# An encoder layer on one core: twelve of the last sixteen block moves issued from GpSimd's queue, and the planner may fill between the row halves of the embedding products

## The chip, the cores and the metric

The kernel runs on one core of a Trainium2 chip. The metric is the device time of one execution in microseconds. Three executions of the kernel before took 1150.88, 1150.77 and 1153.72 us; their median is 1150.88 us.

## The reference, cut to what matters

One layer with S = 256 rows and D = 2048 columns, in float32. Three sub-layers follow each other, each adding to the residual stream h: a mixing part (projections, attention, a recurrent scan, an output projection), a feed-forward part and an embedding part. Only the seam between the last two is touched:

```python
fn = rms_norm(h, g_ffn_pre)
ff = (silu(fn @ w_ffn_gate) * (fn @ w_ffn_up)) @ w_ffn_down
h = h + rms_norm(ff, g_ffn_post)
gate = sigmoid(rms_norm(h, g_ple_pre) @ w_ple_gate)   # 256x2048 times 2048x2048
ple = p @ w_ple_proj                                  # 256x256 times 256x2048
h = h + rms_norm(gate * ple, g_ple_post)
```

## The kernel before, in words

**Products.** Every float32 product is made of three products of split operands: a value is split in a high part (rounded) and a low part (the rest), and hi·hi, lo·hi and hi·lo are summed. A weight tile holds two blocks of 128 rows by 512 columns (512 KB). It is loaded from SyncE's queue into one of four buffers `wr`, ScalarE rounds it to `wh` (L637), VectorE subtracts to `wl` (L650), and TensorE runs 12 matmuls on it: 2 blocks × 2 halves of the rows × 3 products (L684 `wh` with the high part of the activations, L685 `wh` with the low part, L686 `wl` with the high part). A load into `wr` has to wait until the subtraction four tiles earlier has read that buffer; a rounding has to wait until TensorE has finished with the tile four earlier.

**The seam.** After the last feed-forward product come the embedding products for columns 1024 to 2047 (`embedding(2, "sm")` and `embedding(3)`: two tiles of `w_ple_proj`, left operand `pTh`/`pTl`), then the gate products with `w_ple_gate`. The gate's 32 weight tiles are called g0 to g31 in this text. g0 to g15 go in turns over two column chunks: g0 and g1 are the rows 0 to 255 of the weight for chunks 0 and 1, g2 and g3 the next 256 rows, and so on. So g12 to g15 use the last four of the sixteen blocks of the normed activations.

**The normed activations.** The gate's left operand is the transposed residual, times the gain, split in `hT_ffn_hi` (ScalarE, L316) and `hT_ffn_lo` (VectorE, L318), 16 blocks of 128 columns. `next_norm` computes h in pieces of 256 columns for each half of the rows (L1555, sixteen instructions). Blocks 0 to 11 are transposed on TensorE (`transposed`, L329, four matmuls for two blocks) into PSUM. Blocks 12 to 15 take another way (`turn_h`): VectorE transposes them in 32x32 squares into a tile `mid` (L1586), and 16 DMAs of 32 KB each (`moved`, L348) put the squares in their places in a tile `mT`; ScalarE and VectorE then split `mT`. The DMAs run over j (outer) and i (inner), four values each; `pool` lists the values of i whose DMAs GpSimd's queue issues, SyncE's queue issues the rest.

**What sets the order.** The program is written out by a planner. TensorE's main sequence calls `plan.main(cost)` to advance a modelled TensorE clock, and `plan.run()` to emit, in order of modelled start, all side work (roundings, splits, transposes, DMA issues) that would start before that clock. The order of the instructions on each engine is fixed when the program is built; at run time each engine goes through its own list in order and waits where an operand or a buffer is not ready. A queue is an engine's list too: a DMA that has to wait holds up all DMAs behind it on that queue.

Of the kernel before, what the change touches and what calls it, by code (L numbers as in the profile page):

```python
# [18 lines left out]
NT = S // P  # L19
# [61 lines left out]
class Event:  # L81


    t = None
# [141 lines left out]
def dve(n, take=None, give=None):  # L226
    return ("dve", COST["dve"] + 0.00104 * n, None, take, give)
# [11 lines left out]
def layer(ctx: ExitStack, tc: tile.TileContext, a: dict, out: bass.AP):  # L239
# [5 lines left out]
    plan = Plan(wr=R_BUFS, w=W_BUFS, sm=SM_BUFS, acc=4, ev=1, mid=2, bt=2, m2=1, mt=1, sq=1, T0=1, T1=1, T4=1, **{f"{s}{j}": n for s, m, n in (("p", 5, 1), ("t", 3, 0)) for j in range(m)}, wr0=1, w0=1)  # L245
# [52 lines left out]
    def col(name, i):  # L298
        c = VEC_COLS[name][0] + i
        return vec[:, c : c + 1]  # L300
# [13 lines left out]
    def gained_split(hi, lo, src, g, give=None):  # L314
        yield act(S)
        nc.scalar.activation(hi, src, AF.Copy, scale=g)  # L316
        yield dve(S, give=give)
        nc.vector.scalar_tensor_tensor(  # L318
            out=lo, in0=src, scalar=g, in1=f32(hi), op0=ALU.mult, op1=ALU.subtract
        )  # L320
# [11 lines left out]
    def moved(e, here, take, tile_of, turn=True, pool=()):  # L332


        if turn:
            flat = e.rearrange("p t n -> p (t n)")
            yield dve(2 * N)
            nc.vector.transpose(out=flat, in_=flat)
        src = e.rearrange("p t (k j b) -> p t k j b", j=4, b=32)
        mT = None  # L340
        for j in range(4):
            for i in range(4):
                first = None if mT else take
                yield ("pool" if i in pool else "dma", COST["move"], None, first, None)
                if mT is None:
                    mT = tile_of()
                dst = mT.rearrange("p t k (i b) -> p t k i b", b=32)
                (nc.gpsimd if i in pool else nc.sync).dma_start(  # L348
                    dst[32 * j : 32 * j + 32, :, :, i, :],
                    src[32 * i : 32 * i + 32, :, :, j, :],  # L350
                )
        done(here)
        return mT.rearrange("p t k q -> p k t q")
# [16 lines left out]
    def done(event):  # L370
        event.t = plan.now
# [148 lines left out]
    fours = {}  # L520

    raws, his, los = {}, {}, {}
    ev_raw, ev_hi, ev_lo = {}, {}, {}
# [138 lines left out]
    MM = 0.216  # L662
    MM4 = 0.86

    def products(i, kx, lhs, accs, ts, start, stop, *after, seeded=False):
        group = {"skip_group_check": seeded}
        for j in range(2):
            p = (i, j + 1) if (i, j + 1) in ev_lo else (i, 2)
            plan.reach(lhs.ev[kx + j])
            hi, lo = lhs.at[kx + j]  # L670
            st, sp = start and j == 0, stop and j == 1
            if i == 0:
                plan.main(4 * MM, ev_hi[p], lhs.ev[kx + j])
                for t in ts:
                    sl = slice(t * P, (t + 1) * P)
                    nc.tensor.matmul(accs[t], hi[:, sl], his[i][:, j, :], start=st, stop=False, **group)
                    nc.tensor.matmul(accs[t], lo[:, sl], his[i][:, j, :], start=False, stop=False, **group)
                plan.main(2 * MM, ev_lo[p])
            else:
                plan.main(6 * MM * len(ts) / NT, ev_lo[p], lhs.ev[kx + j], *after)  # L680
            for t in ts:
                sl = slice(t * P, (t + 1) * P)
                if i:
                    nc.tensor.matmul(accs[t], hi[:, sl], his[i][:, j, :], start=st, stop=False, **group)  # L684
                    nc.tensor.matmul(accs[t], lo[:, sl], his[i][:, j, :], start=False, stop=False, **group)  # L685
                nc.tensor.matmul(accs[t], hi[:, sl], los[i][:, j, :], start=False, stop=sp, **group)  # L686
            at_pe[0] = max(at_pe[0], i)
            if j:
                free_w(i)
            plan.run()  # L690
# [124 lines left out]
    def free_w(i):  # L815
        if i not in keep:
            plan.free[w_kind(i)].append(plan.clk["pe"])
        if i == max(more_w):
            plan.add(next_gain(("ffn", "g_ffn_post"), plan.clk["pe"]), plan.clk["pe"])

    keep = set()
    def run_seg(s):
        if callable(s[0]):
            s[0](*s[1:])
            return
        chunk, lhs, ks, first, last, after, i0 = s
        if after:
            after()
        if first:
            chunk.open()  # L830
        for n, (_, kx) in enumerate(ks):
            i = i0 + n
            before = [chunk.ready] if first and n == 0 else [chunk.made] if chunk.made else []
            products(i, kx, lhs, chunk.accs, range(NT), first and n == 0,
                     last and n == len(ks) - 1, *before, seeded=bool(chunk.made))
            his.pop(i), los.pop(i)
        if last:
            if chunk.before:
                chunk.before()
            plan.add(chunk.post(chunk), plan.clk["pe"] + plan.SEM, chunk.late)  # L840
            plan.run()
# [584 lines left out]
    pT = [Act(2)] * 2  # L1426
# [96 lines left out]
    def next_norm(sub, nxt, rstd, ev_rstd, g_next):  # L1523
# [24 lines left out]
        for c in range(4):  # L1548
            if c > 1:
                yield nxt.ev[4 * c - 8]  # L1550
            for b in range(2):
                sl = slice(c * N + b * S, c * N + (b + 1) * S)
                for t in range(NT):
                    yield dve(S)
                    nc.vector.scalar_tensor_tensor(  # L1555
                        out=h[:, t, sl], in0=mg[:, t, sl], scalar=ro[:, t : t + 1],
                        in1=h[:, t, sl], op0=ALU.mult, op1=ALU.add,
                    )
                if c < TURNED:
                    plan.add(transpose_h(4 * c + 2 * b, hi, lo, nxt, sub.gname), plan.now)  # L1560
            if c >= TURNED:
                plan.add(turn_h(c, hi, lo, nxt, sub.gname), plan.now, -SOON)
# [17 lines left out]
    def turn_h(c, hi, lo, nxt, gname):  # L1580

        for t in range(NT):
            yield dve(N, take=None if t else "mid")
            if not t:
                e = mid_tile()
            nc.vector.transpose(out=e[:, t, :], in_=t2["h"][:, t, c * N : (c + 1) * N])  # L1586
        there = Event()
        mT = yield from moved(e, there, "mt", mT_tile, turn=False)
        plan.free["mid"].append(plan.now)
        yield there  # L1590
        for b in range(4):
            kk = 4 * c + b
            yield from gained_split(
                *(x[:, kk, :].rearrange("p (t q) -> p t q", t=NT) for x in (hi, lo)), mT[:, b],
                col(gname, kk), give="mt" if b == 3 else None,
            )
            done(nxt.ev[kk])
# [106 lines left out]
    hP = Act()  # L1704
# [16 lines left out]
    def mid_tile():  # L1721
        return t2["pool"].tile([P, NT, N], F32, tag="mid", name="mid", bufs=2)
# [138 lines left out]
    for part, (f0, f1) in enumerate(PARTS):  # L1861
# [11 lines left out]
        for c in range(0, 4, 2):  # L1873
# [11 lines left out]
                after=load_sqrt if end else None,  # L1885
# [172 lines left out]
    n = 0  # L2058
# [47 lines left out]
    with tc.manual_schedule():  # L2106
# [3 lines left out]
        for n, s in enumerate(segs[:-1]):  # L2110
# [3 lines left out]
            if n == n_ffn:  # L2114
                MM = 0.2265
# [7 lines left out]
        chunk, lhs, ks, _, _, _, i0 = segs[-1]  # L2123
        chunk.open()
        for n, (_, kx) in enumerate(ks):
            products(i0 + n, kx, lhs, chunk.accs, [0], n == 0, n == 7, chunk.ready)
# [73 lines left out]
```

## Time and profile before

| what | value |
|---|---|
| three executions, median | 1150.88 us (1150.77 to 1153.72) |
| the profiled execution: time, span of its instructions | 1153.04 us, 1151.0 us |
| TensorE busy, of the span | 1140.0 us, 99% |
| VectorE, ScalarE, GpSimd busy | 79%, 62%, 12% |
| granted TensorE clock, mean | 0.999 |
| bytes moved by DMA | 266.92 MB, mean 232 GB/s |

Times in the views count from the start of the span. Between the profiled execution's own time and its span lie 2.04 us. In the timeline a row is one instruction, or several alike with their count; a bracket at its end gives the idle time of the engine before it and what ended it. Matmuls overlap, so their pace is read from the starts of successive rows and not from their durations. "SPq" and "POOL" rows with DMA_DIRECT2D are issues; the time from an issue to the arrival of its data is given as "DMA to landing".

### The profile page before, as it was taken

The page shows a single profiled execution, that of the slowest core. Times are in us where ns is not written, and L with a number is a line of the kernel's source. Part 1 is how long each engine was busy: PE and PEld are TensorE (multiplying, and loading weights), DVE is VectorE, ACT ScalarE, POOL GpSimd, SP SyncE. Part 2 cuts the span into 40 slices and gives each one's busy share as a digit, 9 for nine tenths or more (in the row PEclk, how much of TensorE's full clock was granted, in tenths as well). Part 3 has the DMA queues.
Part 4 walks back from the last instruction along what each step waited for, and adds up shares of the span by engine and source line. Part 5 has one row for each costly group of instructions (what it writes and reads, how often), then busy time and mean ns, then how long its engine had stood idle before and what let it go on. Part 6 is the DMA issues. An engine that isn't in the chain of part 4 may idle for free.

```text
span 1151.0 us, 15131 instructions
## 1 busy us (share of the span) xinstructions
PE 1140.0 (99%) x5211; PEld 947.9 (82%) x5211; DVE 909.9 (79%) x1143; ACT 714.4 (62%) x948; POOL 135.3 (12%) x216
## 2 busy tenths in 40 slices
PE   9999999999999999999999999999999999999997
PEld 7888888888888888888888888888888888887786
DVE  6578787888458779988787898988888888759574
ACT  6777877875457645656656556565555565556564
POOL 0000000000000033131100123311111303100000
PEclk9999999999999999999999999999999999999999
DMA  9867666546686996876976786887887687965671
GB/s 325 283 191 219 185 185 206 174 148 206 226 285 178 313 296 212 259 199 213 279 253 221 249 237 211 264 254 207 290 291 256 196 264 249 284 237 203 207 246 75
DMA packets 112573, 266.92 MB, mean 232 GB/s; under 512 B 39280, under 2 KB 46192, under 8 KB 111088
## 3 DMA queue, kind: packets, MB, share of 16 engines
q1 hardware_dynamic: 99568, 243.57, 62.8%
q0 software_dynamic: 12496, 22.03, 9.7%
q8 instruction: 41, 0.67, 0.2%
q10 hardware_dynamic: 432, 0.35, 0.1%
q14 instruction: 36, 0.29, 0.1%
HBM read 248.07 MB, written 9.44 MB: 224 GB/s over the span
## 4 chain that ended last, share of the span: by engine, by line
PE 93%; DMA 2%; DVE 2%; ACT 2%; issue 1%; SPq 0%; ACTq 0%; DVEq 0%
PE acc L685 24%; PE acc L686 24%; PE acc L684 24%; PE acc L696 6%; PE acc L695 6%; PE acc L697 6%; PE tr L329 1%; DVE wl L650 1%; ACT wh L637 1%; DMA sq<-ev 0%; DMA mT<-mid 0%; DMA wr<-in_w_ple_gate 0%; PE pg L360 0%; PE pg L361 0%; DMA av<-in_w_rg_i 0%
## 5 line engine op out<-in xcount | busy, mean ns | idle before, releaser
L650 DVE TENSOR_TENSOR wl<-wr,wh 128x1024 fp32r<-128x1024 f32 (+1 forms) x308 | 368.2, 1210 | 106.9 <-ACT wh L637 104.9
L637 ACT CAST wh<-wr 128x1024 fp32r<-128x1024 f32 (+1 forms) x308 | 318.9, 1043 | 198.9 <-PE acc L685 139.2
L685 PE MATMUL acc<-wh,hT_mix_lo 128*128 128x512 f32 x440 | 171.4, 390 | 0.3 <-DVE hT_mix_lo L318 0.3
L684 PE MATMUL acc<-wh,hT_mix_hi 128*128 128x512 f32 x440 | 171.5, 390 | 0.0
L686 PE MATMUL acc<-wl,hT_mix_hi 128*128 128x512 f32 x440 | 171.2, 389 | 0.0
L348 POOL DMA_DIRECT2D mT<-mid x152 | 89.5, 602 | 559.8 <-DMA ple<-in_w_ffn_up 401.2
L686 PE MATMUL acc<-wl,hT_hi 128*128 128x512 f32 x320 | 124.5, 390 | 0.0
L684 PE MATMUL acc<-wh,hT_hi 128*128 128x512 f32 x316 | 124.4, 394 | 0.0
L685 PE MATMUL acc<-wh,hT_lo 128*128 128x512 f32 x316 | 123.1, 390 | 0.0
L637 ACT CAST wh<-ple 128x1024 fp32r<-128x1024 f32 (+1 forms) x61 | 59.8, 982 | 64.5 <-PE acc L685 30.8
L685 PEld LDWEIGHTS acc<-wh,hT_mix_lo 128*128 128x128 f32 x440 | 82.6, 188 | 18.0 <-DVE hT_mix_lo L318 1.0
L686 PEld LDWEIGHTS acc<-wl,hT_mix_hi 128*128 128x128 f32 x440 | 82.6, 188 | 17.1
L684 PEld LDWEIGHTS acc<-wh,hT_mix_hi 128*128 128x128 f32 x440 | 82.6, 188 | 17.0
L650 DVE TENSOR_TENSOR wl<-ple,wh 128x1024 fp32r<-128x1024 f32 (+1 forms) x61 | 69.1, 1133 | 9.3 <-ACT wh L637 8.7
L686 PEld LDWEIGHTS acc<-wl,hT_hi 128*128 128x128 f32 x320 | 60.1, 188 | 12.9
L685 PEld LDWEIGHTS acc<-wh,hT_lo 128*128 128x128 f32 x316 | 59.4, 188 | 11.7
L684 PEld LDWEIGHTS acc<-wh,hT_hi 128*128 128x128 f32 x316 | 59.4, 188 | 11.3
L637 ACT CAST wh<-third 128x1024 fp32r<-128x1024 f32 x32 | 33.6, 1051 | 21.0 <-PE acc L685 18.8
L650 DVE TENSOR_TENSOR wl<-third,wh 128x1024 fp32r<-128x1024 f32 x32 | 39.1, 1221 | 6.8 <-ACT wh L637 6.6
L606 POOL DMA_DIRECT2D ple<-in_w_ffn_up x27 | 24.0, 891 | 163.5 <-DVE wl L650 97.6
L684 PE MATMUL acc<-wh,hT_ffn_hi 128*128 128x512 f32 x104 | 40.9, 393 | 1.5 <-ACT hT_ffn_hi L316 1.5
L685 PE MATMUL acc<-wh,hT_ffn_lo 128*128 128x512 f32 x104 | 40.8, 393 | 0.5 <-DVE hT_ffn_lo L318 0.5
(439 smaller groups left out, 2386.9 us busy)
## 6 DMA issues: line engine op xcount, KB each, us to landing
wr<-in_w_in SPq DMA_DIRECT2D x77, 512.0 KB, 4.5
wr<-in_w_ffn_gate SPq DMA_DIRECT2D x74, 512.0 KB, 5.4
wr<-in_w_ffn_down SPq DMA_DIRECT2D x63, 512.0 KB, 5.2
wr<-in_w_ffn_up SPq DMA_DIRECT2D x49, 512.0 KB, 5.2
wr<-in_w_out SPq DMA_DIRECT2D x32, 512.0 KB, 4.4
wr<-in_w_ple_gate SPq DMA_DIRECT2D x32, 512.0 KB, 4.6
lower<-in_w_ffn_up SPq DMA_DIRECT2D x21, 512.0 KB, 6.1
third<-in_w_ffn_gate SPq DMA_DIRECT2D x14, 512.0 KB, 6.4
```

The lines of the kernel that those rows point to most:

```text
L329: nc.tensor.transpose(tr[:, b, t * P : (t + 1) * P], e[:, t, sl], ident)
L348: (nc.gpsimd if i in pool else nc.sync).dma_start(dst[32 * j : 32 * j + 32, :, :, i, :], src[32 * i : 32 * i + 32, :, :, j, :],)
L606: nc.gpsimd.dma_start(dst, src, accum_op=ALU.add)
L637: nc.scalar.copy(his[i][:, 0 : src.shape[1], :] if n == 2 else his[i][:, j, :], src)
L650: nc.vector.tensor_tensor(out=los[i][:, m, :], in0=src, in1=f32(his[i][:, m, :]), op=ALU.subtract)
L684: nc.tensor.matmul(accs[t], hi[:, sl], his[i][:, j, :], start=st, stop=False, **group)
L685: nc.tensor.matmul(accs[t], lo[:, sl], his[i][:, j, :], start=False, stop=False, **group)
L686: nc.tensor.matmul(accs[t], hi[:, sl], los[i][:, j, :], start=False, stop=sp, **group)
L695: nc.tensor.matmul(dst, x[0], wh, start=start, stop=False, skip_group_check=seeded)
L696: nc.tensor.matmul(dst, x[1], wh, start=False, stop=False, skip_group_check=seeded)
L697: nc.tensor.matmul(dst, x[0], wl, start=False, stop=stop, skip_group_check=seeded)
```

## The change

Two edits. In `turn_h`, where the norm feeds the gate (`nxt is hP`), the 12 DMAs with i = 0, 1, 2 are issued from GpSimd's queue, and only the four with i = 3 stay on SyncE's. The same step of the first norm (`hF`) stays as it was. In `products`, the modelled cost of a block is booked in two halves, one for each half of the rows, and for the embedding products behind the last feed-forward product (`lhs in pT and i > max(fours)`) `plan.run()` is called between the halves, so that side work can be emitted there.

```diff
             else:
-                plan.main(6 * MM * len(ts) / NT, ev_lo[p], lhs.ev[kx + j], *after)
-            for t in ts:
+                plan.main(6 * MM / NT, ev_lo[p], lhs.ev[kx + j], *after)
+            for n, t in enumerate(ts):
+                if i and n:
+                    if lhs in pT and i > max(fours):
+                        plan.run()
+                    plan.main(6 * MM / NT)
                 sl = slice(t * P, (t + 1) * P)
...
         there = Event()
-        mT = yield from moved(e, there, "mt", mT_tile, turn=False)
+        mT = yield from moved(e, there, "mt", mT_tile, turn=False, pool=(0, 1, 2) if nxt is hP else ())
```

The two programs are alike up to the seam. In the changed one, line numbers behind `products` are 4 higher, and what was L1555 is L1559; no computing instruction is added or removed, only the order and the issuing queue change.

SyncE's queue, from the load of the gate gain to the end of the gate's weight loads, before:

```order
L562 DMA wr<-in_w_ple_gate 128x1024 x2
L348 DMA mT<-mid 32x8x32 x3
L562 DMA wr<-in_w_ple_gate 128x1024 x2
L348 DMA mT<-mid 32x8x32
L562 DMA wr<-in_w_ple_gate 128x1024 x3
L348 DMA mT<-mid 32x8x32 x8
L562 DMA wr<-in_w_ple_gate 128x1024 x4
L348 DMA mT<-mid 32x8x32 x3
L562 DMA wr<-in_w_ple_gate 128x1024
L348 DMA mT<-mid 32x8x32
L562 DMA wr<-in_w_ple_gate 128x1024 x15
```

And the same stretch of the changed program:

```order
L562 DMA wr<-in_w_ple_gate 128x1024 x3
L348 DMA mT<-mid 32x8x32
L562 DMA wr<-in_w_ple_gate 128x1024
L348 DMA mT<-mid 32x8x32
L562 DMA wr<-in_w_ple_gate 128x1024 x3
L348 DMA mT<-mid 32x8x32 x2
L562 DMA wr<-in_w_ple_gate 128x1024 x20
```

The first row of each is g5 onwards. The last of the 16 moves stood behind the load of g16 and stands now behind that of g11; between the loads of g11 and g12 stand two moves where there were eight, and none between those of g15 and g17 where there were four. GpSimd's queue ends with 20 moves in a row instead of 8.

VectorE, from the first piece of h in the seam to the first low part of a turned block; before there were six pieces of h ahead of the first `wl` (that of g1), in the changed program three:

```order
L1559 SCALAR_TENSOR_TENSOR h_8470<-mg_8281,ro_ffn,h_8470 128x256
L1559 SCALAR_TENSOR_TENSOR h_8560<-mg_8359,ro_ffn,h_8560 128x256
L1559 SCALAR_TENSOR_TENSOR h_8470<-mg_8281,ro_ffn,h_8470 128x256
L650 TENSOR_TENSOR wl<-wr,wh 128x1024
L1559 SCALAR_TENSOR_TENSOR h_8560<-mg_8359,ro_ffn,h_8560 128x256
L1559 SCALAR_TENSOR_TENSOR h_8470<-mg_8281,ro_ffn,h_8470 128x256
L1559 SCALAR_TENSOR_TENSOR h_8560<-mg_8359,ro_ffn,h_8560 128x256
L318 SCALAR_TENSOR_TENSOR hT_ffn_lo<-tr,vec,hT_ffn_hi 128x256
```

Further on, between the first piece of h and the two 32x32 transposes of `turn_h`, VectorE has now three `wl` and ten low parts where it had two and eight. Behind the transposes the changed program has this (the first four `wl` are those of g4 to g7, the next two those of g8 and g9):

```order
L650 TENSOR_TENSOR wl<-wr,wh 128x1024
L318 SCALAR_TENSOR_TENSOR hT_ffn_lo<-tr,vec,hT_ffn_hi 128x256 x2
L650 TENSOR_TENSOR wl<-wr,wh 128x1024 x3
L1576 TENSOR_REDUCE toth_ffn<-ssh_ffn 128x2
L368 RECIPROCAL rstd_p<-rth_ffn 128x2
L650 TENSOR_TENSOR wl<-wr,wh 128x1024
L318 SCALAR_TENSOR_TENSOR hT_ffn_lo<-mT,vec,hT_ffn_hi 128x256 x3
L650 TENSOR_TENSOR wl<-wr,wh 128x1024
L318 SCALAR_TENSOR_TENSOR hT_ffn_lo<-mT,vec,hT_ffn_hi 128x256
```

Before, the four low parts of `mT` stood behind the `wl` of g13; now three of them stand ahead of the `wl` of g9. On ScalarE, likewise, the first `hT_ffn_hi` from `mT` stood behind the rounding of g13 and stands now ahead of that of g10. On TensorE, the 12 transposes ahead of the first gate matmul are now 8, and the rest stand in groups of 8, 4 and 4 where they stood in groups of 4 and 8; between the embedding products themselves no transpose stands in either program.

## The prediction

> **What bounds the kernel now.** First the page, its busy times and the chain that ended last:
>
> ```profile
> PE 1140.0 (99%) x5211; PEld 947.9 (82%) x5211; DVE 909.9 (79%) x1143; ACT 714.4 (62%) x948; POOL 135.3 (12%) x216
> PE 93%; DMA 2%; DVE 2%; ACT 2%; issue 1%; SPq 0%; ACTq 0%; DVEq 0%
> ```
>
> TensorE is the bound nearly throughout. The change neither adds nor removes a matmul, so all it can save is time in which TensorE waits. The view of waits, for TensorE over the whole span (us in total, times, longest):
>
> ```profile
> PE final L2042 <- ACT diag L2040: 2.0, 1, 2.0
> PE acc L684 <- ACT hT_ffn_hi L316: 1.5, 1, 1.5
> ...
> PE acc L685 <- DVE hT_ffn_lo L318: 0.5, 1, 0.5
> ...
> ```
>
> Two of them lie in the seam: 1.5 us for `hT_ffn_hi` and 0.5 us for `hT_ffn_lo`. The first is the one that the moved DMAs concern. TensorE's timeline at g2 and g12:
>
> ```profile
> 1057.72 0.39 PE L684 MATMUL acc<-wh,hT_ffn_hi 128*128 128x512 f32 x1
> ...
> 1084.73 0.39 PE L686 MATMUL acc<-wl,hT_ffn_hi 128*128 128x512 f32 x1
> 1086.60 0.50 PE L684 MATMUL acc<-wh,hT_ffn_hi 128*128 128x512 f32 x1 [1.48 <-ACT hT_ffn_hi L316]
> 1087.12 0.50 PE L685 MATMUL acc<-wh,hT_ffn_lo 128*128 128x512 f32 x1
> 1087.45 0.39 PE L686 MATMUL acc<-wl,hT_ffn_hi 128*128 128x512 f32 x1
> ```
>
> From 1057.72 to 1084.73 lie 119 matmul steps (g2 to g11 are ten tiles of 12), so a step is 0.227 us and a tile 2.72 us. At that pace the third matmul of g12 would start at 1084.73 + 3 × 0.227 = 1085.41; it starts at 1087.45. The wait thus costs **2.04 us**, the restart of the pipeline included.
>
> Who makes it late? SyncE's queue and ScalarE in the timeline:
>
> ```profile
> 1059.67 1.91 SPq L348 DMA_DIRECT2D mT<-mid  x3
> 1061.69 1.00 SPq L562 DMA_DIRECT2D wr<-in_w_ple_gate  x2
> 1062.74 1.20 SPq L348 DMA_DIRECT2D mT<-mid  x1
> 1064.25 4.28 SPq L562 DMA_DIRECT2D wr<-in_w_ple_gate  x3
> 1068.58 5.94 SPq L348 DMA_DIRECT2D mT<-mid  x8
> 1074.62 2.10 SPq L562 DMA_DIRECT2D wr<-in_w_ple_gate  x4
> 1076.77 1.94 SPq L348 DMA_DIRECT2D mT<-mid  x3
> 1081.07 0.33 SPq L562 DMA_DIRECT2D wr<-in_w_ple_gate  x1
> 1081.45 0.58 SPq L348 DMA_DIRECT2D mT<-mid  x1
> 1086.03 0.91 ACT L316 ACTIVATE hT_ffn_hi<-mT,vec 128x256 fp32r<-128x256 f32 x2 [4.99 <-DMA mT<-mid]
> ```
>
> The 16 moves are issued over 21.8 us, because each weight load between them waits for its buffer. The last leaves at 1081.45, and ScalarE can read `mT` at 1086.03, about 4.5 us later.
>
> **Part 1: the moved DMAs.** The 12 issues on GpSimd's queue depend on no weight load. When are all 16 there? Three terms.
>
> *Start.* The moves wait for VectorE's two 32x32 transposes. Rows of VectorE:
>
> ```profile
> 1046.16 2.46 DVE L1555 SCALAR_TENSOR_TENSOR h<-mg,ro_ffn,h 128x256 f32<-128x256 f32 x6
> 1048.55 1.22 DVE L650 TENSOR_TENSOR wl<-wr,wh 128x1024 fp32r<-128x1024 f32 x1
> 1049.68 0.48 DVE L1555 SCALAR_TENSOR_TENSOR h<-mg,ro_ffn,h 128x256 f32<-128x256 f32 x1
> 1050.08 0.48 DVE L318 SCALAR_TENSOR_TENSOR hT_ffn_lo<-tr,vec,hT_ffn_hi 128x256 fp32r<-128x256 f32 x1
> 1058.33 1.30 DVE L1586 STREAM_TRANSPOSE mid<-h 128x512 f32<-128x512 f32 x2
> ```
>
> From start to start a `wl` takes 1.13 us (1048.55 to 1049.68), a piece of h or a low part 0.40. The changed order puts one more `wl` and two more low parts ahead of the transposes: 1.13 + 2 × 0.40 = 1.93 us. The first move, at 1059.67 before, comes at about 1061.6.
>
> *Issue.* Bursts of moves on GpSimd's queue exist elsewhere in the trace; two of them, each with the time from issue to landing of its moves, and then the DMA share of the windows:
>
> ```profile
> 954.73 2.97 POOL L348 DMA_DIRECT2D mT<-mid  x5 [19.74 <-DVE sums L312]
> 957.90 5.17 POOL L348 DMA_DIRECT2D mT<-mid  x9 [0.20 <-issue]
> ```
>
> ```profile
> DMA to landing us min/median/max: 1.9/4.1/8.3
> ```
>
> ```profile
> 402.93 5.35 POOL L348 DMA_DIRECT2D mT<-mid  x9 [401.17 <-DMA ple<-in_w_ffn_up]
> ...
> 412.32 0.58 POOL L348 DMA_DIRECT2D mT<-mid  x1 [0.78 <-DMA mT<-mid]
> ```
>
> ```profile
> DMA to landing us min/median/max: 4.5/6.9/8.7
> ```
>
> ```profile
> 400.00:420.00 20.00, 20.00 (x90) 16.58 (x89) 15.51 (x18) 9.38 (x10) 10.40 (x17) 1.00 1.01 293
> 953.00:968.00 15.00, 15.00 (x68) 12.43 (x67) 14.12 (x14) 7.76 (x9) 10.33 (x17) 1.00 0.75 221
> 1059.00:1074.00 15.00, 15.00 (x68) 12.32 (x67) 10.78 (x16) 10.89 (x24) 0.00 (x0) 1.00 0.76 224
> ```
>
> The last figure but one is the DMA share: 0.75 in the first burst, 1.01 in the second, and 0.76 before in the window that now takes the moves. In the first burst 14 issues go in 8.3 us, 0.59 each, with no wait to speak of; the 12th leaves 11 × 0.59 = 6.5 us after the first, at 1068.1. In the second, issues wait for the landing of earlier moves, and the 12th leaves 9.4 us after the first (412.32). I take the first, since its DMA share is the same as here.
>
> *Landing.* 4.1 us is the median of the first burst, 6.9 that of the second. I take 5.0, nearer the first, because the weight loads of g9 to g11 fall on the end of the burst. So `mT` is complete at 1068.1 + 5.0 = **1073.1**. The four moves left on SyncE's queue end earlier: the last stands behind the load of g11, issued at the latest in the x3 row of 1064.25, so before 1068.6, plus two issues and 4.5 us, about 1073 too.
>
> g12 needs its first block at 1085, 12 us later. The wait there is gone: **−2.04 us**.
>
> *What is late next.* The planner has put the splits of `mT` early in two lists. On ScalarE the first `hT_ffn_hi` from `mT` stands ahead of the rounding of g10; on VectorE three low parts stand ahead of the `wl` of g9. Both engines stand still until `mT` is complete, and g8 is the last tile that doesn't need them. The cost of each step, from ScalarE's rows (starts: split to rounding 0.41, rounding to split 0.94):
>
> ```profile
> 1087.79 0.50 ACT L316 ACTIVATE hT_ffn_hi<-mT,vec 128x256 fp32r<-128x256 f32 x1
> 1088.20 1.04 ACT L637 CAST wh<-wr 128x1024 fp32r<-128x1024 f32 x1
> 1089.14 0.50 ACT L316 ACTIVATE hT_ffn_hi<-mT,vec 128x256 fp32r<-128x256 f32 x1
> ```
>
> From complete `mT`: split 0.41, rounding of g10 0.94, two splits 0.82, the third low part 0.48, `wl` of g9 1.13, and about 0.3 for the hand-overs between engines: 4.1 us. So `wl` of g9 is there at 1073.1 + 4.1 = 1077.2. g9 starts at 1057.72 + 7 × 2.72 = 1076.8, and its third matmul, the first with `wl`, at 1077.2. It is a dead heat: every microsecond that `mT` is later than 1073.1 becomes a wait of TensorE. I book 0.3 us of wait and 0.3 for the restart (the restart at g12 cost 2.04 − 1.48 = 0.56): **+0.6 us**. Ends: 0 (landing 4.1), and with the second burst's figures 1061.6 + 9.4 + 6.9 + 4.1 = 1082.0, a wait of 4.8 + 0.56 = +5.4 us.
>
> A row against a rule: the issue on SyncE's queue took 21.8 us for 16 moves, more than four times the landing of one. The Trainium skill (DMA: Bandwidth & Descriptors, Issuing engines are not separate DMA queues) says that transfers started by different engines run on the same 16 DMA engines, and that issuing from several saves only issue time, usually small beside the transfer. By that rule nothing would be gained; the rows above disagree on "small", since here the queue holds issues behind waiting loads.
>
> **Part 2: the finer steps of the planner.** No transpose comes to stand between the embedding products, but the orders differ after them. The `wl` of g1 stands 3 × 0.41 = 1.2 us earlier on VectorE, three pieces of h 1.13 us later. TensorE's side:
>
> ```profile
> 1048.40 1.47 PE L329 MATMUL tr<-ident,h 128*128 128x128 f32 x12
> ...
> 1050.61 0.50 PE L685 MATMUL acc<-wh,hT_ffn_lo 128*128 128x512 f32 x1 [0.50 <-DVE hT_ffn_lo L318]
> ```
>
> The first low part now stands behind six pieces of h and one `wl`, 1046.16 + 2.46 + 1.13 = 1049.75, and behind its high part, which ScalarE gives only after the rounding of g3; that rounding waits for the end of the embedding products at 1048.40, so the high part is there at 1048.40 + 0.94 + 0.41 = 1049.75 too. The low part ends near 1050.3 where it ended at 1050.08 + 0.48 = 1050.56, and L685 starts about 0.1 earlier: −0.1. But 16 transposes are then left where 12 were: 4 × 1.47 / 12 = +0.5. From 1050.61 to 1057.72 TensorE has 23 matmuls (5.2 us) and 12 transposes (1.5) in 7.1 us, so 0.4 of gaps; I let half of them close, since the low parts of later blocks now have more transposes ahead of them: −0.2. Net **+0.2 us**, between −0.3 (all gaps close and half of the transposes cost nothing extra) and +0.7 (one more wait of 0.5, like the one now). The rest of what moves is VectorE and ScalarE work that this case gives slack of over a microsecond: the `wl` of g2, behind the low part of block 6, comes near 1056.3 and is read at 1058.2.
>
> **Sum.** −2.04 + 0.6 + 0.2 = −1.2 us. After g12 the program is as before and TensorE is without a wait until `diag`, so the end moves by the same. Profiled: 1153.04 − 1.2 = 1151.8 us. The profiled execution lies 2.16 us above the median of the three runs; against that median the forecast is 1150.88 − 1.2 = **1149.7 us**. 0.3% of it is 3.45 us, about what a measurement of this kernel can tell from no change.
>
> **The rivals.**
>
> *A. The DMA engines hold the moves (0.20).* If the moves share busy engines, issuing earlier brings them no sooner than about 1074.5 to 1075; g9 then waits 1.4 to 1.9 us plus 0.5. For it: the share of 0.98 in the middle of the window,
>
> ```profile
> 1064.00:1069.00 5.00, 5.00 (x24) 4.14 (x23) 2.94 (x4) 3.93 (x12) 0.00 (x0) 1.00 0.98 346
> ```
>
> against it, the median of 4.1 us at a share of 0.75. It gives −2.04 + 2.2 + 0.2 = +0.4: 1151.3 us. This is also what is left of the rule above.
>
> *B. Slower: a new wait at g9 (0.15).* The mechanism is the split of `mT` standing ahead of g9's `wl`. It decides from `mT` complete at 1075.0 on. With the second burst's waits between issues and its landing, 1077.9, the sum is +5.4 − 2.04 + 0.2 = +3.6: 1154.5 us. Two thirds of this case lie above 0.3%.
>
> *C. The runs without a profile don't have the wait at g12 (0.14).* Their median is 2.16 us under the profiled execution, as much as the wait costs; with moves landing 2 us sooner it would be gone already. Then nothing is gained and the seam costs 0 to +0.8: about 1151.2 us. Against it: one of the three runs, 1153.72, is as slow as the profiled one, so the difference can have any origin.
>
> *D. More is gained than the waits show (0.03).* All waits of the seam with restarts and gaps are about 3.4 us; that would reach 1147.5 us.
>
> The forecast (−2.4 to −0.5) has 0.48. Range: from 1148.3 (no new wait, and the seam 0.5 better) to 1153.6, which takes in A, C and the lower part of B and leaves out about 0.12 above and 0.05 below. Faster by over 0.3%: 0.03 (D); slower: 0.10 (two thirds of B); within: 0.87.
>
> **What would show it.** Right: no wait of TensorE for `hT_ffn_hi` at g12, the first L348 of the seam on GpSimd near 1061.6, the last near 1068, the first split of `mT` near 1073, g9 with a wait under 1 us. Wrong: a wait of L686 for `wl` of over 2 us at g9 or g10, issues on GpSimd with idle times for earlier moves, or a span that is unchanged though TensorE waits less.

## The result, and the profile after

Over nine executions each, the kernel before has a median of 1151.96 us (1150.56 to 1153.72) and the changed kernel 1154.91 us (1152.92 to 1156.78). The ratio is 1.0023, 95% interval 1.0014 to 1.0032: the change makes the kernel slower, by 3 us. The prediction, 1149.7 us, a little faster, was wrong, and the result lies outside its range.

The profiled execution of the changed kernel is the fastest of the nine: 1152.92 us, span 1151.1 us. It reached the seam 0.62 us sooner than the profiled one of before (the first transposes behind the embedding products start at 1047.78 and 1048.40 us), so differences are taken from that point on.

The page's busy times of the changed kernel; the computing engines do what they did, GpSimd has the twelve issues more:

```profile
PE 1140.0 (99%) x5211; PEld 948.6 (82%) x5211; DVE 909.0 (79%) x1143; ACT 715.0 (62%) x948; POOL 142.2 (12%) x228
```

The waits of TensorE over the whole span, changed kernel (lines of `products` are 4 higher, so L688 to L690 were L684 to L686):

```profile
PE acc L690 <- DVE wl L650: 2.4, 1, 2.4
PE final L2046 <- ACT diag L2044: 2.0, 1, 2.0
...
```

The wait of 1.5 us for `hT_ffn_hi` at g12 is gone. A wait of 2.4 us for `wl` has come. TensorE's timeline shows its place:

```profile
1047.78 1.17 PE L329 MATMUL tr<-ident,h 128*128 128x128 f32 x8
1049.22 0.50 PE L688 MATMUL acc<-wh,hT_ffn_hi 128*128 128x512 f32 x1 [0.27 <-ACT hT_ffn_hi L316]
...
1056.93 0.40 PE L688 MATMUL acc<-wh,hT_ffn_hi 128*128 128x512 f32 x1
...
1076.21 0.39 PE L689 MATMUL acc<-wh,hT_ffn_lo 128*128 128x512 f32 x1
1078.99 0.50 PE L690 MATMUL acc<-wl,hT_ffn_hi 128*128 128x512 f32 x1 [2.39 <-DVE wl L650]
...
1141.87 1.02 PE L2141 MATMUL final<-h,ident 128*128 128x512 f32 x2
```

The row of 1056.93 is the first matmul of g2. Seven tiles of 2.72 us later is 1075.97, where g9 starts, so 1078.99 is the third matmul of g9, the first with g9's `wl`. It should have followed 0.23 us after 1076.21; the delay is 2.55 us. Now the issues of the changed kernel, SyncE's queue:

```profile
1060.68 0.60 SPq L348 DMA_DIRECT2D mT<-mid  x1
...
1063.70 2.61 SPq L562 DMA_DIRECT2D wr<-in_w_ple_gate  x3
1066.36 1.26 SPq L348 DMA_DIRECT2D mT<-mid  x2
1070.52 27.11 SPq L562 DMA_DIRECT2D wr<-in_w_ple_gate  x11
```

and GpSimd's:

```profile
1061.22 0.59 POOL L348 DMA_DIRECT2D mT<-mid  x1 [69.81 <-ACT wh L637]
1061.99 4.59 POOL L348 DMA_DIRECT2D mT<-mid  x8 [0.18 <-issue]
1067.17 1.73 POOL L348 DMA_DIRECT2D mT<-mid  x3 [0.59 <-DMA mT<-mid]
```

The sixteen moves leave between 1060.7 and 1068.3, where the last left at 1081.45 before. Three answers on the tile `mT` give their landing: the first is over all sixteen, the second over the last two of SyncE's queue (issued at 1066.4 and 1067.0), the third over the last three of GpSimd's (1067.2 to 1068.3):

```profile
DMA to landing us min/median/max: 2.7/5.9/8.2
```

```profile
DMA to landing us min/median/max: 7.8/8.0/8.2
```

```profile
DMA to landing us min/median/max: 6.1/6.5/6.9
```

Both queues end together: 1067.0 + 7.8 = 1074.8 and 1068.3 + 6.1 to 6.9 = 1074.4 to 1075.2 (the split below starts at 1075.03). The windows around it, in the columns used in the prediction:

```profile
1060.00:1065.00 5.00, 5.00 (x24) 4.14 (x23) 5.00 (x8) 3.94 (x9) 3.60 (x7) 1.00 0.82 215
1065.00:1070.00 5.00, 5.00 (x24) 4.14 (x23) 2.01 (x4) 4.77 (x13) 3.31 (x6) 1.00 1.05 287
1070.00:1075.00 5.00, 5.00 (x24) 4.14 (x23) 0.50 (x1) 0.19 (x1) 0.00 (x0) 1.00 0.96 236
```

The DMA engines are full or nearly so from 1065 to 1075 (shares of 1.05 and 0.96), and from 1070 on VectorE (0.50 us busy of 5) and ScalarE (0.19) stand still. What they do next, ScalarE and then VectorE:

```profile
1068.20 1.99 ACT L637 CAST wh<-wr 128x1024 fp32r<-128x1024 f32 x2
1075.03 0.51 ACT L316 ACTIVATE hT_ffn_hi<-mT,vec 128x256 fp32r<-128x256 f32 x1 [4.84 <-DMA wr<-in_w_ple_gate]
1075.45 1.03 ACT L637 CAST wh<-wr 128x1024 fp32r<-128x1024 f32 x1
1076.39 0.90 ACT L316 ACTIVATE hT_ffn_hi<-mT,vec 128x256 fp32r<-128x256 f32 x2
```

```profile
1069.27 1.23 DVE L650 TENSOR_TENSOR wl<-wr,wh 128x1024 fp32r<-128x1024 f32 x1 [0.78 <-ACT wh L637]
...
1076.92 0.89 DVE L318 SCALAR_TENSOR_TENSOR hT_ffn_lo<-mT,vec,hT_ffn_hi 128x256 fp32r<-128x256 f32 x2 [0.86 <-ACT hT_ffn_hi L316]
1077.72 1.22 DVE L650 TENSOR_TENSOR wl<-wr,wh 128x1024 fp32r<-128x1024 f32 x1
```

ScalarE has both roundings, g8 and g9, done at 1070.2 and then stands in front of the first split of `mT` for 4.8 us. VectorE is free for g9's `wl` from about 1070.5; it stands behind three low parts of `mT` and starts at 1077.72. TensorE gets it at 1078.99.

From the first transposes to the end, the rows give: seam front 9.15 us to the first matmul of g2 where it took 9.32, −0.17; g12, −2.04; g9, +2.55. That is +0.3 us. The whole stretch, to the first of the `final` matmuls at the end, took 94.09 us where it took 93.66 (1142.06 in the trace of before): +0.4. The two profiled executions agree (−0.12 us in time, +0.62 for the earlier arrival: +0.5). The medians differ by 2.95 us: the profiled execution of before lies 1.1 us above its kernel's median, and that of the changed kernel 2.0 below. So what costs most lies in executions that were not profiled. The mean granted clocks of the changed kernel's nine say where to look: the three with 0.998 took 1152.92, 1153.52 and 1153.90 us, the six with 0.997 or 0.996 took 1154.56 to 1156.78.

### The profile page after: what moved, and what is told of

The parts are those of the page before. It is cut to its first block, busy times and chain, and to the rows that moved or that the text cites. A ratio compares the mean times of both kernels' runs of the same rounds, so it can differ in the third digit from the quotient of the medians.

```text
span 1151.1 us, 15145 instructions
## 1 busy us (share of the span) xinstructions
PE 1140.0 (99%) x5211; PEld 948.6 (82%) x5211; DVE 909.0 (79%) x1143; ACT 715.0 (62%) x948; POOL 142.2 (12%) x228
## 4 chain that ended last, share of the span: by engine, by line
PE 96%; DVE 1%; ACT 1%; DMA 1%; issue 0%; POOL 0%; ACTq 0%; POOLq 0%
PE acc L690 25%; PE acc L689 25%; PE acc L688 25%; PE acc L700 6%; PE acc L701 6%; PE acc L699 6%; PE tr L329 1%; DMA wr<-in_w_ple_gate 1%; PE warm L2113 0%; DVE wl L650 0%; DVE hT_ffn_lo L318 0%; ACT wh L637 0%; DVE h L1559 0%; PE pg L360 0%; PE pg L361 0%; PE pg L359 0%
## 5 line engine op out<-in xcount | busy, mean ns | idle before, releaser
L348 POOL DMA_DIRECT2D mT<-mid x164 | 96.3, 600 | 627.5 <-ACT wh L637 470.4
L688 PE MATMUL acc<-wh,hT_mix_hi 128*128 128x512 f32 x440 | 171.5, 390 | 0.0
L690 PE MATMUL acc<-wl,hT_mix_hi 128*128 128x512 f32 x440 | 171.2, 389 | 0.0
L690 PE MATMUL acc<-wl,hT_hi 128*128 128x512 f32 x320 | 124.5, 390 | 0.0
L688 PE MATMUL acc<-wh,hT_hi 128*128 128x512 f32 x316 | 124.4, 394 | 0.0
L690 PEld LDWEIGHTS acc<-wl,hT_mix_hi 128*128 128x128 f32 x440 | 82.6, 188 | 17.1
L688 PEld LDWEIGHTS acc<-wh,hT_mix_hi 128*128 128x128 f32 x440 | 82.6, 188 | 16.9
L690 PEld LDWEIGHTS acc<-wl,hT_hi 128*128 128x128 f32 x320 | 60.1, 188 | 12.8
L688 PEld LDWEIGHTS acc<-wh,hT_hi 128*128 128x128 f32 x316 | 59.4, 188 | 11.5
L690 PE MATMUL acc<-wl,hT_ffn_hi 128*128 128x512 f32 x104 | 40.6, 391 | 2.4 <-DVE wl L650 2.4
L688 PE MATMUL acc<-wh,hT_ffn_hi 128*128 128x512 f32 x104 | 40.9, 393 | 0.3 <-ACT hT_ffn_hi L316 0.3
```

The lines of the kernel that those rows point to most:

```text
L348: (nc.gpsimd if i in pool else nc.sync).dma_start(dst[32 * j : 32 * j + 32, :, :, i, :], src[32 * i : 32 * i + 32, :, :, j, :],)
```

## The experiments

The theory has three parts. First, the change loses time at g9 because the splits of `mT` stand ahead of g9's `wl`, and nowhere else. Second, the idle time of TensorE there, 2.4 us and more, costs more than itself when the granted clock falls. Third, `mT` lands late because the moves share busy DMA engines with the weight loads. The rivals: the finer steps of the planner cost the time by the order of other work; the loss is only the wait; and GpSimd's own issue path makes the landing slow.

**The changed kernel again**, `after_again`, without an edit:

> The changed kernel once more, for a second profile and on the same chip as the next three. Theory 1 (order): the splits of mT stand ahead of g9's wl on VectorE and of g10's rounding on ScalarE, mT is complete about 1075, and TensorE waits at g9 for wl; 1.0015 to 1.0035 of before. Its nine executions had mean clocks of 0.996 to 0.998, where the profile shown had 0.998 and a wait of 2.4 us: if the granted clock falls after a longer wait, a profile with 0.996 shows a stretch of half clock behind g9, some 5 us long, that costs 2 to 3 us more. Theory 2 (queue): the moves on GpSimd's queue make the weight loads land later, and the waits lie at g11 to g13 for weights. Then the wait at g9 would be no larger in a slower run.

It took 1155.17 us (1153.19 to 1157.23, 7 executions), ratio 1.0027 (1.0016 to 1.0038). TensorE at g9:

```profile
1079.36 0.50 PE L690 MATMUL acc<-wl,hT_ffn_hi 128*128 128x512 f32 x1 [2.75 <-DVE wl L650]
```

The wait is there again, 0.4 us longer. The profiled execution is again the fastest, and again the time goes roughly with the mean clock: 0.998 took 1153.19, 0.997 took 1155.17, 0.996 took 1154.46 to 1157.13, 0.995 took 1157.01 and 1157.23 us. Eight of the sixteen executions in these two runs have 0.995 or 0.996; apart from `early2` below, no execution of another kernel whose clock is on record has less than 0.997.

**The splits of `mT` placed later**, `late4`. The planner books the arrival of `mT` 4 us later; issues, loads and computing instructions are those of the changed kernel:

```diff
         yield there
+        if nxt is hP:
+            plan.now += 4.0
+            late = Event()
+            done(late)
+            yield late
```

On VectorE `wl` of g9, g10 and g11 then stand ahead of the four low parts of `mT`, on ScalarE the roundings of g10 and g11 ahead of all four high parts.

> The changed kernel, with the splits of mT put 4 us later in the planner, so that they stand behind the wl and the rounding of g11; every other row of VectorE, ScalarE and SyncE stands as in the changed kernel. Theory 1: the wait at g9 is gone and none comes at g12, TensorE waits in the seam for under 0.6 us; 1.5 to 2.5 us faster than before (0.9978 to 0.9987), 4 to 5 us faster than the changed kernel. Theory 2: the moves still share the DMA engines with the loads, waits for weights remain, and it is no faster than before (1.000 to 1.002).

It took 1150.66 us (1150.01 to 1151.77, 11 executions), ratio to before 0.9986 (0.9977 to 0.9994), 4.5 us below the changed kernel on the same chip. ScalarE's split, and the landing of the moves:

```profile
1076.24 1.71 ACT L316 ACTIVATE hT_ffn_hi<-mT,vec 128x256 fp32r<-128x256 f32 x4 [0.23 <-DMA wr<-in_w_ple_gate]
```

```profile
DMA to landing us min/median/max: 2.8/5.6/8.7
```

And TensorE's first transposes behind the embedding products, and the first `final` matmul:

```profile
1048.41 1.17 PE L329 MATMUL tr<-ident,h 128*128 128x128 f32 x8
...
1139.83 1.02 PE L2146 MATMUL final<-h,ident 128*128 128x512 f32 x2
```

The moves land as slowly as in the changed kernel (5.6 us median and 5.9). The high parts are done at 1077.95, almost 7 us before g12 (ten tiles of 2.72 us behind g2, which starts at 1057.58) needs them, and TensorE waits neither at g9 nor at g12. The stretch between the two rows takes 91.42 us, 2.7 us less than in the changed kernel. The whole loss of the change, and the gain meant for it, hang on where the splits stand.

**The DMA move alone**, `pool_only` (the edit in `products` undone):

```diff
-                plan.main(6 * MM / NT, ev_lo[p], lhs.ev[kx + j], *after)
-            for n, t in enumerate(ts):
-                if i and n:
-                    if lhs in pT and i > max(fours):
-                        plan.run()
-                    plan.main(6 * MM / NT)
+                plan.main(6 * MM * len(ts) / NT, ev_lo[p], lhs.ev[kx + j], *after)
+            for t in ts:
```

> Only the first edit: the 12 moves on GpSimd's queue, the planner as before. On VectorE one split of mT stands ahead of g9's wl instead of three, two ahead of g10's, and the 32x32 transposes stand as early as before. Theory 1: mT is complete near 1073.5, g9's wl is 2.2 us behind it, in time for 1077.2; no wait over 0.5 us at g9; 1.5 to 2 us faster than before (0.998 to 0.999). Theory 2: as slow as the changed kernel (1.002).

It took 1152.30 us (1151.38 to 1153.82, 11), ratio 0.9999 (0.999 to 1.0008). SyncE's queue, GpSimd's queue, ScalarE and TensorE:

```profile
1065.60 4.76 SPq L562 DMA_DIRECT2D wr<-in_w_ple_gate  x3
1070.41 1.26 SPq L348 DMA_DIRECT2D mT<-mid  x2
...
1068.22 1.16 POOL L348 DMA_DIRECT2D mT<-mid  x2 [1.38 <-DMA mT<-mid]
1070.37 0.58 POOL L348 DMA_DIRECT2D mT<-mid  x1 [0.99 <-DMA mT<-mid]
...
1077.95 0.51 ACT L316 ACTIVATE hT_ffn_hi<-mT,vec 128x256 fp32r<-128x256 f32 x1 [3.35 <-DMA mT<-mid]
...
1080.17 0.50 PE L686 MATMUL acc<-wl,hT_ffn_hi 128*128 128x512 f32 x1 [1.47 <-DVE wl L650]
```

The expectation on `mT` missed: it was complete at 1077.95, 4.4 us later than expected; 1.26 us of this is a later arrival at the seam (its first transposes start at 1049.66), and 3.2 us is later counted from there. The last two moves on SyncE's queue stand behind three loads and leave only from 1070.41 on, and GpSimd's issues wait 1.38 and 0.99 us for earlier moves to land. The new wait at g9 is there too, but 0.9 us shorter, although `mT` came later: one split of `mT` stands ahead of g9's `wl`, not three, and the `wl` follows complete `mT` by 2.2 us instead of 4.0. It takes back most of what the wait at g12 gave, and the time shows no difference from before.

**The finer planning alone**, `plan_only` (all sixteen moves on SyncE's queue):

```diff
-        mT = yield from moved(e, there, "mt", mT_tile, turn=False, pool=(0, 1, 2) if nxt is hP else ())
+        mT = yield from moved(e, there, "mt", mT_tile, turn=False)
```

> Only the second edit: the finer planning, all 16 moves on SyncE's queue. The last two moves stand behind the load of g16, the splits of mT behind g14. Theory 1: the wait at g12 for hT_ffn_hi stays, a little longer than before because two moves instead of one stand last: 1.5 to 2.5 us; same as before to 0.1% slower (0.9995 to 1.001). Theory 3 (the finer planning itself makes the seam slower): 1.002, with the loss ahead of g2.

It took 1152.34 us (1151.54 to 1154.29, 11), ratio 1.0004 (0.9995 to 1.0013): no difference from before. TensorE waits at g12 as it did before, for 1.92 us where it was 1.48:

```profile
1087.16 0.50 PE L688 MATMUL acc<-wh,hT_ffn_hi 128*128 128x512 f32 x1 [1.92 <-ACT hT_ffn_hi L316]
```

By itself this edit costs nothing that can be measured. Together with the moves it helps to put the splits where they do harm.

**The moves alone with later splits**, `pool_late4` (the edits of `pool_only` and `late4` together):

> Only the first edit, with the splits of mT put 4 us later: behind g11 on VectorE and ScalarE. Theory 1: no wait at g10 or g12; only the old 0.5 us ahead of the first gate matmul stays. 1.5 to 2 us faster than before (0.998 to 0.999), the same as late4 to 0.5 us: the gain is that of the queue, and the finer planning adds next to nothing. Theory 3 (the finer planning is what makes late4 fast): 1.000.

It took 1150.50 us (1149.48 to 1151.71, 11), ratio 0.9987 (0.9978 to 0.9996), within 0.2 us of `late4`. The finer steps are not needed for the gain.

**TensorE kept busy through the wait**, `fill12`. Twelve matmuls of g9's own operands into a spare bank stand ahead of the first matmul with g9's `wl`:

```diff
+                if i == i_ple + 9 and j == 0 and t == 0:
+                    spare = bank("spare").rearrange("p k s -> p (k s)")
+                    for _ in range(12):
+                        nc.tensor.matmul(spare, hi[:, sl], his[i][:, j, :], start=True, stop=True)
```

> The changed kernel with 12 more matmuls ahead of the first matmul of g9 that reads wl (same operands as the one before, into a PSUM bank that nobody reads): 2.7 us of work for TensorE where it now waits 2.4 to 2.7 us in the profiles and, as the executions without a stored trace suggest, longer. Theory 1a (the wait's cost is doubled by the granted clock, which falls after a long idle time): the time stays at the changed kernel's fastest, 1152.9 to 1153.7, and the clocks of all executions are 0.997 to 0.999; median 1.5 to 2 us below the changed kernel. Theory 1b (only the wait itself varies): no faster than the changed kernel, 1155 to 1156, clocks 0.996.

It took 1153.75 us (1153.23 to 1155.97, 11), ratio 1.0016 (1.0007 to 1.0025). The twelve matmuls take 12 × 0.227 = 2.72 us, as long as the wait, and TensorE no longer waits for `wl`. Still its median is 1.2 to 1.4 us below those of the changed kernel, a little less than the 1.5 to 2 us expected, and all its executions have a mean clock of 0.997 or 0.998. Idle time of TensorE thus seems to have cost more than the same time filled with work. By the times alone this is a hint only, since the intervals of the ratios overlap (1.0007 to 1.0025 here, 1.0014 to 1.0032 and 1.0016 to 1.0038 there); the next run shows the price itself.

**The splits placed earlier still**, `early2` (the planner books `mT` 2 us sooner, with `there.t -= 2.0` ahead of `yield there`):

> The changed kernel with the splits of mT put 2 us earlier in the planner: all four low parts stand ahead of g8's wl on VectorE, one high part ahead of g9's rounding. Theory 1: mT is complete at 1075 to 1075.5 as before, g8's wl follows 5.2 us later, at 1080.5, where it is needed at 1074.2; TensorE waits about 6 us at g8, 3.5 us longer than in the changed kernel's profile. Theory 1a: the granted clock falls to a half in this wait and stays there some us behind it, and the time is 1158 to 1160; theory 1b: 1156.5 to 1157.5 with the clock at full. Theory 2 (the moves slow the weight loads, the order of the splits is no matter): 1155.

It took 1157.85 us (1157.64 to 1158.91, 5), ratio 1.0054 (1.0042 to 1.0067). That lies between the two times expected, with a clock that falls (1158 to 1160) and with a full one (to 1157.5), so the trace has to decide. TensorE around the wait, which now falls on g8:

```profile
1073.30 0.39 PE L689 MATMUL acc<-wh,hT_ffn_lo 128*128 128x512 f32 x1
1080.01 0.80 PE L690 MATMUL acc<-wl,hT_ffn_hi 128*128 128x512 f32 x1 [6.32 <-DVE wl L650]
1080.60 0.63 PE L688 MATMUL acc<-wh,hT_ffn_hi 128*128 128x512 f32 x1
1081.03 0.63 PE L689 MATMUL acc<-wh,hT_ffn_lo 128*128 128x512 f32 x1
...
1083.16 0.40 PE L688 MATMUL acc<-wh,hT_ffn_hi 128*128 128x512 f32 x1
1083.40 0.40 PE L689 MATMUL acc<-wh,hT_ffn_lo 128*128 128x512 f32 x1
```

Windows of the same stretch, TensorE alone (length, busy time and count, granted clock, DMA share, GB/s):

```profile
1075.00:1076.00 1.00, 0.00 (x0) 1.00 0.00 0
1076.00:1077.00 1.00, 0.00 (x0) 0.67 0.00 0
1077.00:1078.00 1.00, 0.00 (x0) 0.50 0.00 0
...
1082.00:1083.00 1.00, 1.00 (x4) 0.50 0.92 315
1083.00:1084.00 1.00, 1.00 (x5) 0.92 0.82 242
```

Here the second part of the theory is seen in a trace. TensorE's last matmul ahead of the wait ends at 1073.69. The clock falls to 0.50 at about 1076.34, 2.65 us later (0.67 in the second window is a third of it at full clock). After the restart at 1080.01 the matmuls come every 0.43 us instead of 0.23, until 1083.16, when the full clock is back, 3.15 us after the restart. The seven steps of that stretch, the restart included, take 3.15 us where at full clock they would take about 1.7: **1.5 us** on top of the wait.

The waits of the changed kernel are shorter than that one. Whether they can bring the clock down is shown by a wait that all ten traces share: TensorE stands still for 2.04 us ahead of its last two matmuls (`final<-mg,diag`). In `pool_only`:

```profile
1146.10 1.93 PE L2042 MATMUL final<-mg,diag 128*128 128x512 f32 x2 [2.04 <-ACT diag L2040]
```

```profile
1146.00:1148.00 2.00, 1.90 (x2) 0.36 (x2) 1.72 (x3) 0.04 (x1) 0.00 (x0) 0.57 0.37 138
```

In the kernel before:

```profile
1145.12 1.12 PE L2042 MATMUL final<-mg,diag 128*128 128x512 f32 x2 [2.04 <-ACT diag L2040]
```

In `pool_only` the clock falls at 1146.28 (0.57 in the window), 0.18 us after the wait has ended, and the two matmuls take 1.93 us; in the kernel before it stays full until 1147.85, and they take 1.12 us. So a wait of 2.04 us can bring the clock down, and doesn't always. `early2` shows why. Its clock falls once more at the end, at 1151.44:

```profile
1150.00:1152.00 2.00, 1.13 (x2) 0.30 (x2) 1.74 (x3) 0.65 (x2) 0.00 (x0) 0.86 0.36 136
```

From the first fall (1076.34) to the return (1083.16) lie 6.82 us, and from there to the second fall 68.28 us: 2 and 20 times 3.41. So in this trace the clock changes only at the ends of windows of 3.41 us. In `pool_only` the 3.41 us ahead of the fall hold the whole wait of 2.04 us. In `after_again` the clock falls at the end at 1145.86; twenty windows earlier, at 1077.6, a window ended inside the wait at g9 and cut it into 1.0 and 1.76 us, and the clock stayed full. In these traces, then, 2.04 us of idle time in one window were enough and 1.76 were not. If the wait lies anywhere in the windows with equal chance, one of 2.39 to 2.75 us puts over 1.76 to 2.04 us into a single window in half to three quarters of the executions (an estimate from these figures).

The Trainium skill (TensorE: Matmul & The Clock Gate, Part 1) has this as a rule: the activity of TensorE is watched in a free-running window of about 3.4 us, an idle window halves the clock, and about 3.4 us of sustained work bring it back. The traces agree on the window and on the return (3.15 us of work in `early2`), but the window need not be idle throughout, since 2.04 us of 3.41 were enough.

The two profiled executions of the changed kernel kept their full clock behind g9. That others lost it isn't shown by a trace of them; it follows from their mean clocks, from `fill12` and from these windows.

**No weight loads beside the moves**, `quiet2`. The loads of g8 to g31 are left out, and their roundings read a tile that is already there:

```diff
                 yield dma(256 * n, take=None if j.start else raw_kind(i))
+                if i >= i_ple + 8:
+                    raws[i] = t2["third"]
+                    done(ev_raw[i, j.stop])
+                    continue
```

> The changed kernel without the weight loads of g8 to g31 (24 loads of 512 KB left out; these tiles are rounded from data already on the chip, so every instruction of ScalarE, VectorE and TensorE stays, in the same order). The twelve moves on GpSimd's queue then have the DMA engines to themselves from about 1063. Theory 3a, the weight loads beside the moves set their landing (6.7 us from the 12th issue instead of 5.0): issues still leave at 0.58 us each, the median landing falls to 4.1 us or less, mT is complete at 1071 to 1073, the wait for wl at g9 falls under 0.5 us, and the time comes to about 1150.5 to 1152. Theory 3b, the path of GpSimd's own queue sets it, whatever else the DMA engines do: landing stays near 6 to 7 us, the splits of mT stay at about 1075, the wait stays at 2.4 to 2.8 us and the time at 1153 to 1155.

It took 1150.35 us (1149.85 to 1152.15, 10), ratio 0.999 (0.998 to 1.0). GpSimd's issues, ScalarE's first split (line numbers 4 higher), and the landing of the sixteen moves:

```profile
1061.40 0.59 POOL L348 DMA_DIRECT2D mT<-mid  x1 [69.48 <-ACT wh L641]
1062.16 6.34 POOL L348 DMA_DIRECT2D mT<-mid  x11 [0.18 <-issue]
...
1070.59 0.51 ACT L316 ACTIVATE hT_ffn_hi<-mT,vec 128x256 fp32r<-128x256 f32 x1
```

```profile
DMA to landing us min/median/max: 1.8/2.1/3.5
```

The issues leave at the same pace, 0.58 us each; the last leaves at 1067.9, in the changed kernel at 1068.3. The landing falls from a median of 5.9 us to 2.1. ScalarE doesn't wait for `mT` at all, and no wait of TensorE at g9 is left. The weight loads on the same DMA engines set the landing; GpSimd's path doesn't.

## Why the prediction was wrong, point by point

**The failed step: the landing.** The prediction chose the first burst for the issue because the window of before had a DMA share of 0.76, like that burst's 0.75, and put the landing at 5.0 us, nearer that burst's 4.1. In the changed kernel the share is 1.05 and 0.96 where the last moves fly, and the last ones took 6.1 to 8.2 us. Counted from the first transposes of the seam, `mT` was booked complete at 24.7 us (1073.1 − 1048.40) and was complete at 27.25 (1075.03 − 1047.78), 2.55 us late. The start has 0.2 us of this, the issue 0.6 and the landing behind the twelfth issue 1.7 (6.7 us instead of 5.0). The share of before was the wrong one to go by: the moves were then spread over 21.8 us. That drawing them together raised the share is likely and not shown by itself. The prediction had the rows for this: 0.98 in the middle of the window, and 6.9 us at a share of 1.01. The last two moves on SyncE's queue were booked at about 1073 and missed in the same way, with 7.8 to 8.2 us.

**The term that followed from it: the new wait.** It was booked at 0.3 us plus 0.3 and measured 2.39 to 2.75, a delay of 2.55 to 2.9 us. The mechanism and its place were right: from complete `mT` to g9's `wl` the prediction had 4.1 us, and the rows give 1075.03 to 1078.99, 4.0 us. That each microsecond of lateness becomes one of waiting held as well: 2.55 us of lateness, counted from the seam, became 2.55 us of delay. Rival B named exactly this, with 1075.0 as the point from which it decides, and it had 0.15. Rival A, the full DMA engines, is what brought it about; it gave +0.4 and 1151.3 us, which is what the rows show and not what the medians show.

**The price that was missing: the granted clock.** From the rows the sum is +0.3 to +0.7 us, near rival A's +0.4, and within the range. The medians say +3. Nothing in the prediction charged TensorE's idle time more than its length and a restart. The rule of the Trainium skill quoted above (TensorE: Matmul & The Clock Gate, Part 1), which asks for an idle window of about 3.4 us, would not have charged a wait of 2.4 us either. `early2` shows the price where it is paid, 1.5 us; `fill12` recovers 1.2 to 1.4. The account is clearest against `late4`, which has the same moves and ran on the same chip as `after_again`. From the first transposes to the first `final` matmul the rows give 91.42 us there and 94.09 and 94.43 in the two traces of the changed kernel, 2.7 to 3.0 more; the medians differ by 4.5. The 1.5 to 1.8 us between them are what the fallen clock cost in `early2`. About 0.5 us stays open on the other side: against before, the rows of `late4` and `pool_late4` give −2.24 and −2.06 us, their medians −1.67 and −1.53. In `fill12`, which kept its clock, some 1.2 us stay open (+0.5 by its rows, +1.7 by its median).

**What was right.** The wait at g12 is gone in full (−2.04 us). The issue came near what was booked: 7.1 us from the first to the twelfth on GpSimd's queue (1061.22 to 1068.3) where 6.5 were booked; the difference is one wait of 0.59 us for an earlier move to land, which the prediction had named as a sign of being wrong. The seam's front was booked at +0.2 us, between −0.3 and +0.7, and came to −0.17; `plan_only` shows no cost of it. Rival C, that executions without a profile lack the wait at g12, falls in the main: `late4` and `pool_late4`, whose rows lack that wait and have no new one, gain 1.7 and 1.5 us over before. The 0.5 us that they gain less than their rows say could be what is left of it. The Trainium skill's rule quoted in the prediction (DMA: Bandwidth & Descriptors, Issuing engines are not separate DMA queues) holds for the landing: the issue got 14 us shorter, and the moves still shared 16 engines with the loads, as `quiet2` shows.

## What to carry to other kernels

A transfer that arrives earlier is also consumed earlier in lists written ahead of time, so look at what stands behind its consumers there; placing the same splits 4 us later turned a loss of 3 us into a gain of 1.5 to 1.7. Take the landing of a burst from the DMA share that the window will have with the burst in it, not from the share before. And treat a wait of TensorE of 2 us and more as possibly dearer than its length, and compare the mean granted clock of all executions, since the profiled one may be the one that escaped.

## What was not expected of the hardware

The granted clock can fall for a wait of 2.04 us (`pool_only`) and stay full through one of 2.75 us (`after_again`): what counts in these traces is how much of the wait falls into one window of 3.41 us. One kernel's executions so spread from 1152.92 to 1157.23 us, at mean clocks of 0.998 down to 0.995. And 512 KB loads in flight beside them made moves of 32 KB land in 5.9 us instead of 2.1, at an unchanged issue rate.
